# S5 stage of a decoder step: output-side complex products accumulated on TensorE, doubled columns for B and C, x scaled on ScalarE

## The chip, the cores and the metric

The kernel runs on 1 core of one Trainium2 chip, in one launch. Its time is the device time of one execution in microseconds (us). The core has five engines that run side by side, each with its own instruction queue: TensorE (PE, matrix products and transposes), VectorE (DVE), ScalarE (ACT), GpSimd (POOL) and SyncE (SP, which here only issues transfers). They wait for one another through semaphores.

## The reference, cut to what matters

One inference step of a decoder over 256 prompt tokens and 8 sequences of 8 new tokens (320 tokens in all, width 1024). The first layer is an S5 layer: a complex diagonal state space for each of 64 groups of 16 channels, with 64 states to a group. Later parts (memory attention, a squared-ReLU MLP, a latent-attention layer, another memory attention and MLP) are not touched.

```python
def s5_mixer(u, a_re, a_im, log_dt, b_re, b_im, c_re, c_im, d_skip, w_glu, h0_re, h0_im):
    ...
    mag = jnp.exp(ar * dt)
    abar_re = mag * jnp.cos(ai * dt)
    abar_im = mag * jnp.sin(ai * dt)
    ...
    bbar_re = coef_re[..., None] * br - coef_im[..., None] * bi
    bbar_im = coef_re[..., None] * bi + coef_im[..., None] * br
    bu_re = jnp.einsum('gnk,btgk->btgn', bbar_re, ug)
    bu_im = jnp.einsum('gnk,btgk->btgn', bbar_im, ug)
    ...
    _, _, h_re, h_im = lax.associative_scan(
        _complex_affine_combine, (a_seq_re, a_seq_im, bu_re, bu_im), axis=1)
    y = jnp.einsum('gkn,btgn->btgk', cr, h_re) - jnp.einsum('gkn,btgn->btgk', ci, h_im)
    y = y.reshape(bsz, t, dm) + d_skip.astype(f32) * u.astype(f32)
    g = jax.nn.gelu(y, approximate=False).astype(u.dtype)
    z = g @ w_glu
    out = z[..., :dm] * jax.nn.sigmoid(z[..., dm:])
    return out, h_re[:, -1], h_im[:, -1]
```

Beside it stands `mem_kv`, which projects 256 memory tokens to keys and values of the first layer (`mn @ w_k`, `mn @ w_v`); it depends on nothing of the S5 layer.

## The kernel before, in words

The 320 tokens are cut into chunks of L = 8 steps, which gives NCH = 40 chunks. Inside a chunk the state space is written out as matrix products; between chunks a scan carries the state. The 64 groups are worked in four quarters (`hq` 0 to 3) of 16 groups each, with an upper and a lower half (`hh`) on partitions 0 to 63 and 64 to 127.

**Parameters.** `natb` and `natc` hold B and C by rows. `transposed` (L818) turns them by TensorE into `bcps` and writes them out as `m_b` and `m_c`, with halves copied by ScalarE (L827) and VectorE (L829 to L834). The input `xc` is scaled by `rC` on VectorE (L804, four tiles `xr`), turned (`ups`) and kept as `U`.

**State side** (`state_side`, L879): for each quarter and half, two products and a sum on VectorE (L885 to L887, tiles `tq`), a column of it kept in `bz` by ScalarE (L889), transposes `rps`, their copies `rt` by ScalarE (L894), and 32 small products `sps` with `U`, which ScalarE copies into the scan's array `H` (L904, L905).

**Output side** (`out_side`, L908): for each quarter and half, two products and a sum on VectorE, `ca` or for the third quarter `hca` (L923), `ct` (L924) and their sum (L925); `ct` has one buffer. TensorE multiplies the sum with `bz` (`kps`, L932), ScalarE copies it out as `kk` (L935), VectorE adds the diagonal `dd` (L941), and eight transfers of the SP queue spread `kk` over a tile `tt` (L944).

**Scan** (`scan`, L948): `scan(0)` works on the first two quarters, `scan(1)` on the last two. Each is a tree of small operations on VectorE (`sc` and `H`, L961 to L967), and ends with copies into the tile `HS` (L982, L984 on VectorE, the rest on ScalarE). Here HS(0) and HS(1) are these two tiles.

**Outputs** (`outputs`, L987): for each quarter 16 pairs of products, `yps<-tt,U` (L999) and `yps<-ca,HS` (L1001), then transposes `ytp`, a Gelu, and a split into `xh` and `xl`, the inputs of the GLU. The GLU is a product with `w_glu` in three matmuls a piece (L204 to L206) on chunks of weights: `wraw` is loaded by the SP queue (L183), ScalarE makes `whi` of it (L190) and VectorE `wlo` (L191). After the GLU come the sigmoid and the product `y` (L649). `fps` are transposes for the final states; `kn`, `kt` and `xps` belong to what follows the GLU.

**Fillers.** `mem_kv` of the first layer is 128 matmuls of 256 columns (L567, L569, `mm<-mnp,...`) whose weights lie raw in the three weight rings `raw`, `hi` and `lo` of `weight_buffers`, without being split; each ring has two buffers of one pool, listed twice, and a third one from the pool `wg`, which opens after `mem_kv`.

The instructions of an engine run in the order in which they were queued. That order is not the order of the code: a scheduler decides it when the program is built, from the dependencies, the buffers that come free and its own estimates. So an edit in one place can move work of another.

Of the kernel before, what the change touches and what calls it, by code (L numbers as in the profile page):

```python
# [88 lines left out]
class Trunk:  # L89
# [76 lines left out]

    def weight_buffers(self, third):
        self.wring = {k: [(self.wp, 2), (self.wp, 2), (third, 1)] for k in ('raw', 'hi', 'lo')}

# [8 lines left out]
    def load_chunk(self, srcs, cols):  # L178
# [13 lines left out]
        return hi, lo  # L192

    def load_plain(self, src):

        kind = ('raw', 'hi', 'lo')[self.plain % 3]
        self.plain += 1
        raw = self.wtile(kind, F32)
        self.last_w = self.nc.sync.dma_start(raw.rearrange("p (k c) -> p k c", c=256), src)
        return raw  # L200
# [188 lines left out]
    def load_gains(self, pool):  # L389
        nc, I, cp = self.nc, self.I, self.cp  # L390
        self.gT = cp.tile([128, 128], F32, name="gT")
        gn = pool.tile([109, 128], F32, name="gn")
        for i, g in enumerate(GAINS):
            nc.sync.dma_start(gn[i * 16:(i + 1) * 16, :], I[g].rearrange("l (j p) -> (l j) p", p=128))
        nc.sync.dma_start(gn[96:104, :], I['kv_in_norm'].rearrange("(j p) -> j p", p=128))
        nc.sync.dma_start(gn[104:106, :], I['kv_latent_norm'].rearrange("(j p) -> j p", p=128))
        nc.sync.dma_start(gn[106:109, :], I['q_norm'].rearrange("l (j p) -> (l j) p", p=128))
        ps = self.ps_mm.tile([128, 512], F32, name="gps", tag="mm")
        self.transpose(ps[:, :109], gn)
        nc.vector.tensor_copy(self.gT[:, :109], ps[:, :109])  # L400
# [147 lines left out]
    def mem_kv(self, l, op, x):  # L548
# [6 lines left out]
        for g in range(8):  # L555
            W, c0 = (Wk, g * 256) if g < 4 else (Wv, (g - 4) * 256)
            ps = [self.ps_mm.tile([128, 512], F32, name="mm", tag="mm") for _ in range(2)]
            for k0 in range(0, KD, 4):
# [13 lines left out]
                for kk in range(4):  # L572
                    k = k0 + kk
                    for b in range(2):
# [3 lines left out]
                        else:  # L578
                            s = slice(kk * 256, (kk + 1) * 256)
                            ms = slice(b * 128, (b + 1) * 128)  # L580
                            self.mm3(ps[b][:, :256], xh[:, k, ms], xl[:, k, ms], hi[:, s], lo[:, s], k == 0, k == KD - 1)
            t = op.tile([128, 512], F32, name="kvo", bufs=1)
            if g < 4:
# [28 lines left out]
    def s5(self, mkv):  # L612
        sp, close_sp = self.open("s5")
        mn, close_mn = self.open("memn0", side="right")
        mx = self.mem_x(mn, plain=True)
        self.rB = mn.tile([128, MT], F32, name="rB")
        close_s8 = self.s5_scan(sp, mkv, mx)
        for unit, _ in enumerate(self.mem_kv(0, mkv, mx)):
            if unit == 0:
                with self.tc.issue_after(self.last_w.ins):  # L620
                    self.load_gains(sp)
        close_mn()
        wg, self.close_wg = self.open("wglu", side="right")
        self.weight_buffers(wg)
        close_s8()
        close_sp()
# [32 lines left out]
    def s5_scan(self, sp, mkv, mx):  # L659
# [15 lines left out]
        for i in range(2):  # L675
# [6 lines left out]
        bn = xp.tile([2 * G, 1024], F32, name="bn", tag="xr", bufs=2)  # L682
        nat = {'b': pp.tile([2 * G, (K + 1) * N], F32, name="natb"),
               'c': self.xp.tile([2 * G, (K + 1) * N], F32, name="natc", tag="xl", padded_shape=[128, 2560])}

# [8 lines left out]
        for i in range(2):  # L694
            cols = slice(i * D // 2, (i + 1) * D // 2)
            nc.sync.dma_start(xc[i * NCH:i * NCH + NC_P], I['x_prompt'][0].rearrange("(c s) d -> c s d", s=L)[:, :, cols])
            nc.sync.dma_start(xc[i * NCH + NC_P:(i + 1) * NCH], I['x_sample'][:, :, cols])
        load_nat('c', nat['c'][:, :K * N])
        V.tensor_copy(an[:, 2], ld[:, :, None].to_broadcast([G, 2, N]))

        V.tensor_mul(nat['b'][:, :K * N].rearrange("p (k n) -> p n k", k=K),
                             bn.rearrange("p (n k) -> p n k", k=K), gxn[:, None, :].to_broadcast([2 * G, N, K]))
        for t in nat.values():
            V.tensor_copy(t[:, K * N:], t[:, :N])
        V.tensor_mul(dn, dn, gxn[:G])
# [80 lines left out]
        self.par_done = V.tensor_sub(rev(QY), T1, T2)  # L786
        a8n = sp.tile([128, 2, G], F32, name="a8n")
        A.activation(a8n[:, 0], PR[:, 8], AF.Copy)
# [13 lines left out]
        for fb in range(4):  # L802
            xr = xp.tile([2 * NCH, 8, L, K], F32, name="xr", bufs=2)
            V.tensor_mul(xr, xc[:, :, fb * 128:(fb + 1) * 128].rearrange("p s (g k) -> p g s k", k=K),  # L804
                                 rC[:, None, :, None].to_broadcast([2 * NCH, 8, L, K]))
            for half in range(2):
# [10 lines left out]

        def transposed(c):  # L818
            t = nat[c]
            ev = mat[c].rearrange("p r g (k o) -> p o k r g", o=2)  # L820
            for o in range(2):
                for x0 in (0, 4):
                    p = tp("bcps")
                    for x in range(4):
                        self.transpose(p[:, x * 128:(x + 1) * 128], t[:, (2 * (x0 + x) + o) * N:(2 * (x0 + x) + o + 2) * N])
                    v = p.rearrange("p (k r g) -> p k r g", k=4, r=2)
                    A.activation(ev[top, o, x0:x0 + 4], v[top], AF.Copy)  # L827
                    if o == 0:
                        V.tensor_copy(ev[bot, 1, x0:x0 + 4], v[bot])  # L829
                    elif x0 == 0:  # L830
                        V.tensor_copy(ev[bot, 0, 1:5], v[bot])
                    else:
                        V.tensor_copy(ev[bot, 0, 5:], v[bot, :3])
                        V.tensor_copy(ev[bot, 0, 0], v[bot, 3])  # L834
# [73 lines left out]
        def out_side(hq):  # L908
            ca = []
            E = V  # L910
            if hq == 2:
                big = self.hp.tile([128, 2, 8, 9, K], F32, name="hca", tag="h", padded_shape=[128, 2, 8, 10, K])
            for hh in range(2):
# [7 lines left out]
                A.activation(c[bot, :, 0], CI[bot, gs], AF.Copy, scale=-1.0)  # L921
                t1 = s8.tile([128, 8, L, K], F32, name="ct", bufs=1)
                E.tensor_mul(c[:, :, 1:], b4(CR, gs), q4(X1, gs))  # L923
                E.tensor_mul(t1, b4(CI, gs), q4(Y1, gs))  # L924
                E.tensor_add(c[:, :, 1:], c[:, :, 1:], t1)  # L925

            kk = s8.tile([K, L, 16, K], F32, name="kk", tag="kk", bufs=1)
            ps = at("kps")
            for j in range(4):
                for q in range(4):  # L930
                    u = q * 4 + j
                    nc.tensor.matmul(ps[q * 32:q * 32 + K, j * 128:(j + 1) * 128], bz[:, (hq * 16 + u) * K:(hq * 16 + u + 1) * K],  # L932
                                     ca[u // 8][:, u % 8, 0:L, :], start=True, stop=True, skip_group_check=True)
            for q in range(4):
# [8 lines left out]
            for s in range(L):  # L943
                nc.sync.dma_start(tt[s * K:(s + 1) * K, s:], kk[:, 0:L - s])  # L944
            return ca, tt

# [856 lines left out]
```

## Time and profile before

| quantity | value |
|---|---|
| time, median of 3 runs | 1229.59 us (1228.91 to 1232.15) |
| the profiled execution's own time | 1235.15 us |
| its span, first to last instruction | 1233.5 us |
| mean granted TensorE clock | 0.966 of full speed |
| busy share of TensorE, VectorE, ScalarE, GpSimd | 92%, 59%, 44%, 15% |
| the S5 stage with its GLU | the first 229.7 us of the span |

The busy shares are means over the whole span and hide how the first stage differs: there TensorE waits for VectorE, while from some 150 us on it is nearly always busy. The rows below are from that stage. In a timeline row the first number is the start, the second the time from the first to the last end of the group; a bracket names the idle time of the engine just before it and what ended that time.

### The profile page before, as it was taken

How to read it: one execution, taken by the hardware profiler on the slowest of the kernel's cores; microseconds unless marked ns; L12 is line 12 of the kernel's file. 1: busy time of each engine (PE TensorE's matmuls, PEld its weight loads, DVE VectorE, ACT ScalarE, POOL GpSimd, SP SyncE). 2: the span in 40 equal slices, each digit the busy share in tenths (PEclk: the TensorE clock that was granted, in tenths of full speed). 3: DMA queues.
4: the chain of work that ended last, by engine and by line, in shares of the span. 5: the costliest groups of instructions: out<-in, count | busy, mean ns of one | idle time of the engine just before them, and what ended most of it. 6: DMA issues, size and time to landing. Idle time of an engine off the chain costs nothing.

```text
span 1233.5 us, 21037 instructions
## 1 busy us (share of the span) xinstructions
PE 1139.3 (92%) x8105; PEld 1026.6 (83%) x8105; DVE 726.7 (59%) x1266; ACT 546.7 (44%) x992; POOL 182.3 (15%) x190
## 2 busy tenths in 40 slices
PE   4997699889988999999989999998999899999996
PEld 3886599776787999999979984578967899999996
DVE  5998944664468553564587674416843685435543
ACT  6344454534444543453366353224443365335541
POOL 2000000350027000000050054202700140000011
PEclk8999799999998999999999999989999999999998
DMA  8535358637334445454443565437272434454441
GB/s 165 180 100 116 72 118 289 245 120 269 124 103 126 137 154 153 143 151 152 154 143 104 170 185 153 140 137 268 84 272 94 137 99 144 151 153 139 155 149 49
DMA packets 151233, 184.84 MB, mean 150 GB/s; under 512 B 16719, under 2 KB 119388, under 8 KB 151068
## 3 DMA queue, kind: packets, MB, share of 16 engines
q1 hardware_dynamic: 141660, 174.84, 46.3%
q10 hardware_dynamic: 6976, 5.46, 1.4%
q0 software_dynamic: 2496, 3.20, 0.9%
q8 instruction: 64, 1.05, 0.3%
q14 instruction: 37, 0.30, 0.1%
HBM read 174.89 MB, written 6.21 MB: 147 GB/s over the span
## 4 chain that ended last, share of the span: by engine, by line
PE 75%; DVE 10%; DMA 5%; SPq 3%; issue 2%; ACT 2%; POOL 2%; POOLq 0%; DVEq 0%; ACTq 0%
PE mm L205 17%; PE mm L204 17%; PE mm L206 17%; PE kt L102 2%; PE sps L1182 2%; PE mm L567 2%; DVE xl L279 2%; PE s L1662 2%; SPq L944 2%; DVE wlo L191 1%; DMA natc<-in_ssm_c_im 1%; PE pov L1239 1%; PE s L1703 1%; PE pps L1217 1%; PE mm L569 1%
## 5 line engine op out<-in xcount | busy, mean ns | idle before, releaser
L191 DVE TENSOR_TENSOR wlo<-wraw,whi 128x1024 fp32r<-128x1024 f32 (+1 forms) x206 | 252.9, 1232 | 279.3 <-ACT whi L190 269.1
L190 ACT ACTIVATE whi<-wraw 128x1024 fp32r<-128x1024 f32 (+1 forms) x216 | 224.5, 1044 | 302.8 <-PE mm L205 246.6
L205 PE MATMUL mm<-xl,whi 128*128 128x320 f32 x944 | 296.8, 317 | 9.1 <-DVE xl L279 7.0
L204 PE MATMUL mm<-xh,whi 128*128 128x320 f32 x944 | 280.6, 318 | 12.7 <-ACT t_up L1295 3.6
L206 PE MATMUL mm<-xh,wlo 128*128 128x320 f32 x944 | 287.3, 314 | 0.0
L205 PEld LDWEIGHTS mm<-xl,whi 128*128 128x128 f32 x944 | 181.8, 193 | 13.7 <-DVE xl L279 9.6
L204 PEld LDWEIGHTS mm<-xh,whi 128*128 128x128 f32 x944 | 175.9, 192 | 16.8 <-ACT t_up L1295 3.9
L206 PEld LDWEIGHTS mm<-xh,wlo 128*128 128x128 f32 x944 | 179.7, 192 | 0.1
L204 PE MATMUL mm<-hh,whi 128*128 128x320 f32 x512 | 158.2, 309 | 0.0
L205 PE MATMUL mm<-hl,whi 128*128 128x320 f32 x512 | 158.0, 309 | 0.0
L206 PE MATMUL mm<-hh,wlo 128*128 128x320 f32 x512 | 157.1, 308 | 0.0
L205 PEld LDWEIGHTS mm<-hl,whi 128*128 128x128 f32 x512 | 96.1, 188 | 0.0
L204 PEld LDWEIGHTS mm<-hh,whi 128*128 128x128 f32 x512 | 96.1, 188 | 0.0
L206 PEld LDWEIGHTS mm<-hh,wlo 128*128 128x128 f32 x512 | 95.9, 188 | 0.0
L118 POOL TENSOR_TENSOR sq<-sq 128x320 f32<-128x320 f32 x34 | 41.4, 1219 | 204.1 <-ACT sq L120 203.4
L191 POOL TENSOR_TENSOR wlo<-wraw,whi 128x1024 fp32r<-128x1024 f32 x10 | 25.4, 2538 | 286.4 <-ACT whi L190 198.1
L102 PEld LDWEIGHTS kt<-ident,kn 128*128 128x128 f32 x256 | 28.9, 143 | 22.2 <-issue 5.8
L102 PE MATMUL kt<-ident,kn 128*128 128x128 f32 x256 | 38.1, 283 | 8.6 <-ACT ktb L1109 3.2
L1591 POOL DMA_DIRECT2D rop<-in_cache_k_rope x64 | 34.5, 540 | 37.4 <-issue 20.4
L256 POOL TENSOR_TENSOR t_up<-y,rr 128x320 f32<-128x320 f32 x6 | 7.5, 1258 | 219.2 <-DVE h L257 219.2
L1107 DVE COPY ktb<-kt 128x512 f32<-128x512 f32 x32 | 22.0, 687 | 21.0 <-PE kt L102 20.9
L1109 ACT ACTIVATE ktb<-kt 128x512 f32<-128x512 f32 x32 | 19.1, 596 | 31.4 <-PE kt L102 26.0
(495 smaller groups left out, 1958.6 us busy)
## 6 DMA issues: line engine op xcount, KB each, us to landing
wraw<-in_w_mlp_up SPq DMA_DIRECT2D x64, 512.0 KB, 4.2
wraw<-in_w_mlp_down SPq DMA_DIRECT2D x64, 512.0 KB, 3.5
kn<-in_cache_mem_k SPq DMA_DIRECT2D x16, 1024.0 KB, 7.3
vn<-in_cache_mem_v SPq DMA_DIRECT2D x16, 1024.0 KB, 9.1
wraw<-in_w_glu SPq DMA_DIRECT2D x32, 256.0 KB, 4.1
wraw<-in_w_mem_q SPq DMA_DIRECT2D x16, 512.0 KB, 5.3
wraw<-in_w_mem_o SPq DMA_DIRECT2D x16, 512.0 KB, 5.0
lat<-in_cache_kv_latent SPq DMA_DIRECT2D x64, 128.0 KB, 2.5
```

The lines of the kernel that those rows point to most:

```text
L102: self.nc.tensor.transpose(out, in_, self.ident[b:b + k, b:b + k])
L118: eng.tensor_add(st['acc'], st['acc'], st['last'])
L190: nc.scalar.activation(hi[:, :cols], raw[:, :cols], AF.Copy)
L191: (nc.gpsimd if self.chunk in POOL_LO else nc.vector).tensor_sub(lo[:, :cols], raw[:, :cols], hi[:, :cols].bitcast(F32))
L204: nc.tensor.matmul(ps, wh, xh, start=start, stop=False)
L205: nc.tensor.matmul(ps, wh, xl, start=False, stop=False)
L206: nc.tensor.matmul(ps, wl, xh, start=False, stop=stop)
L279: lo = nc.vector.scalar_tensor_tensor(xl[:, j, :], s, gpre(j), xh[:, j, :].bitcast(F32), op0=ALU.mult, op1=ALU.subtract)
L567: nc.tensor.matmul(ps[b][:, :MT], w[:, bs], xh[:, k, :], start=k == 0, stop=k == KD - 1)
L944: nc.sync.dma_start(tt[s * K:(s + 1) * K, s:], kk[:, 0:L - s])
L1182: nc.tensor.matmul(sps[h * 32:(h + 1) * 32, :MT], qm[:, h * 2 + db, j * 128 + i * 32:j * 128 + (i + 1) * 32], ktb[:, h * 2 + db, :], start ...
L1591: last[eng] = eng.dma_start(dst, src[bass.ds(v, 1)].rearrange("o p d -> (o p) d"))
```

## The change

Four things are edited.

1. On the output side the sum of the two products is no longer formed. `ca` and `ct` stay as two tiles (`ct` with four buffers), and each of the two users multiplies twice into the same PSUM tile: `kps` has a second matmul of 112 columns with `ct`, and `yps` a third pair, `yps<-ct,HS`.
2. `natb` and `natc` are laid out with each column block twice, so that a transpose gives both halves on all 128 partitions, and ScalarE copies them out in 8 pieces instead of VectorE and ScalarE in halves. C is loaded into a tile `cn` first and then copied into `natc`, once by VectorE and once by ScalarE.
3. `xr` is scaled by 32 ScalarE instructions of 80 x 128 instead of four VectorE ones of 80 x 1024.
4. The staging tile `kvo` of `mem_kv` takes a buffer of a weight ring (`plain_tile`; it shows as `wlo` in the rows of the change), and the rings get a third buffer for `raw` and `hi` only.

```diff
-    def weight_buffers(self, third):
-        self.wring = {k: [(self.wp, 2), (self.wp, 2), (third, 1)] for k in ('raw', 'hi', 'lo')}
+    def weight_buffers(self, third, kinds=('raw', 'hi', 'lo')):
+        self.wring = {k: [(self.wp, 2), (self.wp, 2)] + [(third, 1)] * (k in kinds) for k in ('raw', 'hi', 'lo')}
...
-            t = op.tile([128, 512], F32, name="kvo", bufs=1)
+            t = op.tile([128, 512], F32, name="kvo", bufs=1) if l else self.plain_tile()
...
-        self.weight_buffers(wg)
+        self.weight_buffers(wg, ('raw', 'hi'))
...
+        A.activation(nat['b'][:, :, 1], nat['b'][:, :, 0], AF.Copy)
...
-            V.tensor_mul(xr, xc[:, :, fb * 128:(fb + 1) * 128].rearrange("p s (g k) -> p g s k", k=K),
-                                 rC[:, None, :, None].to_broadcast([2 * NCH, 8, L, K]))
+            for i in range(L):
+                A.activation(xr[:, :, i], xc[:, i, fb * 128:(fb + 1) * 128].rearrange("p (g k) -> p g k", k=K),
+                             AF.Copy, scale=rC[:, i:i + 1])
...
+            ev = mat[c].rearrange("p r g k -> p k r g")
+            for k0 in range(0, K, 4):
+                p = tp("bcps")
+                for x in range(4):
+                    self.transpose(p[:, x * 128:(x + 1) * 128],
+                                   t[:, k0 + x].rearrange("p o n -> p (o n)"))
+                v = p.rearrange("p (k r g) -> p k r g", k=4, r=2)
+                A.activation(ev[:, k0:k0 + 4], v, AF.Copy)
...
+        V.tensor_copy(nat['c'][:, :, 0], cnv)
+        A.activation(nat['c'][:, :, 1], cnv, AF.Copy)
...
-                t1 = s8.tile([128, 8, L, K], F32, name="ct", bufs=1)
+                t1 = s8.tile([128, 8, L, K], F32, name="ct", bufs=4)
+                cb_.append(t1)
                 E.tensor_mul(c[:, :, 1:], b4(CR, gs), q4(X1, gs))
                 E.tensor_mul(t1, b4(CI, gs), q4(Y1, gs))
-                E.tensor_add(c[:, :, 1:], c[:, :, 1:], t1)
...
-                                     ca[u // 8][:, u % 8, 0:L, :], start=True, stop=True, skip_group_check=True)
+                                     ca[u // 8][:, u % 8, 0:L, :], start=True, stop=False, skip_group_check=True)
+                    nc.tensor.matmul(ps[q * 32:q * 32 + K, j * 128 + K:(j + 1) * 128], bz[:, (hq * 16 + u) * K:(hq * 16 + u + 1) * K],
+                                     cb_[u // 8][:, u % 8, 0:L - 1, :], start=False, stop=True, skip_group_check=True)
...
-                    for st in range(2):
+                    for st in range(3):
...
-                                nc.tensor.matmul(o, HS[:, g2 * NCH:g2 * NCH + 64], ca[hh][:, gl, 1:, :], start=False, stop=True)
+                                m = ca[hh][:, gl, 1:, :] if st == 1 else cb_[hh][:, gl]
+                                nc.tensor.matmul(o, HS[:, g2 * NCH:g2 * NCH + 64], m, start=False, stop=st == 2)
```

The scheduler answers with another order of the whole first stage. Three places of it follow; the line numbers of the change are 2 to 5 higher than those before.

On VectorE, at the start of `scan(0)`, the kernel before queues scan operations, the sums into `ca`, the additions to `kk` and the state side of the last quarters in turn:

```order
L923 TENSOR_TENSOR ca<-m_c,X_211 128x8x128
L982 COPY HS<-H 64x16x8
L984 COPY HS<-H 64x16x8
L925 TENSOR_TENSOR ca<-ca,ct 128x8x128
L965 TENSOR_TENSOR sc<-sc 128x256
L965 TENSOR_TENSOR sc<-sc 128x16x8
L941 TENSOR_TENSOR kk<-kk,dd 16x128 x2
L886 TENSOR_TENSOR tq<-m_b,QY 128x1024
L924 TENSOR_TENSOR ct<-m_c,Y_212 128x1024
```

In the change the state side runs ahead of the scan, and the four `ct` tiles of the first two quarters are made in one go just before it:

```order
L888 TENSOR_TENSOR tq<-m_b,QY 128x1024
L889 TENSOR_TENSOR tq<-tq 128x1024
L887 TENSOR_TENSOR tq<-m_b,QX 128x1024
L869 MEMSET H 128x64
L927 TENSOR_TENSOR ct<-m_c,Y_212 128x1024 x2
L944 TENSOR_TENSOR dd<-dT,ident 16x128 x2
L927 TENSOR_TENSOR ct<-m_c,Y_212 128x1024 x2
L981 MEMSET HS 128x24
L591 TENSOR_TENSOR kt<-mm,rB 128x256
L926 TENSOR_TENSOR ca<-m_c,X_211 128x8x128
```

Of the seven `ct` and six sums that stood ahead of HS(0), four `ct` are left there; the third quarter's two `ct` now stand near the end of `scan(1)`, 68 rows after HS(0).

On TensorE, behind the outputs of the second quarter, the kernel before goes on with the GLU:

```order
L1001 MATMUL yps<-ca,HS 64x128 x2
L999 MATMUL yps<-tt,U 64x128 x2
L1001 MATMUL yps<-ca,HS 64x128 x2
L204 MATMUL mm<-xh,whi 128x320 x4
L932 MATMUL kps<-ca,bz 16x128 x2
L205 MATMUL mm<-xl,whi 128x320
L206 MATMUL mm<-xh,wlo 128x320
```

In the change matmuls of `mem_kv` stand between the outputs instead. This is the place behind the first quarter's outputs, where the `kps` of the third quarter needs its `ct`:

```order
L1006 MATMUL yps<-ct,HS 64x128 x2
L934 MATMUL kps<-hca,bz 16x128
L572 MATMUL mm<-whi,mnp 128x256 x7
L572 MATMUL mm<-wraw,mnp 128x256 x5
L102 MATMUL ytp<-ident,yc 128x128 x8
L1003 MATMUL yps<-tt,U 64x128 x2
L1006 MATMUL yps<-ca,HS 64x128 x2
L936 MATMUL kps<-ct,bz 16x112
```

And this is where the GLU begins, behind the last matmuls of `mem_kv`:

```order
L1006 MATMUL yps<-ct,HS 64x128 x2
L572 MATMUL mm<-wraw,mnp 128x256 x3
L572 MATMUL mm<-whi,mnp 128x256 x8
L102 MATMUL ytp<-ident,yc 128x128 x8
L102 MATMUL fps<-ident,H 32x128
L102 MATMUL fps<-ident,F 32x128 x8
L207 MATMUL mm<-xh,whi 128x320
L208 MATMUL mm<-xl,whi 128x320
```

In the kernel before all 128 matmuls of `mem_kv` stand ahead of the first `yps<-ca,HS`; in the change 73 do, and 55 behind it (12, then 18, 14 and 11 between the outputs), and no matmul of the GLU is left between the outputs.

On the SP queue the kernel before has two of the transfers of `w_glu` behind the `tt` of the first quarter, and ten behind those of the second:

```order
L944 DMA tt<-kk 16x768
L944 DMA tt<-kk 16x512
L944 DMA tt<-kk 16x256
L183 DMA wraw<-in_w_glu 128x2x256 x10
L944 DMA tt<-kk 16x2048
L944 DMA tt<-kk 16x1792
```

In the change (with buffer numbers) all of them stand behind the last `tt`, and the chunk 1877, which the GLU multiplies first, behind 1908 and 1939:

```order
L948 DMA tt_242<-kk_1246 16x512
L948 DMA tt_242<-kk_1246 16x256
L183 DMA wraw_1908<-in_w_glu 128x2x256 x2
L183 DMA wraw_1939<-in_w_glu 128x2x256 x2
L183 DMA wraw_1877<-in_w_glu 128x2x256 x2
```

Each of these three waits for TensorE to be done with the matmuls of `mem_kv` that read the buffer before.

## Rows read from the trace of the kernel before

**Rows 1.** Windows of core 0: length, busy us of each engine (instructions), PEclk, DMA
```profile
25.20:131.90 106.70, 88.92 (x734) 75.48 (x735) 98.24 (x211) 47.55 (x114) 0.00 (x0) 0.92 0.49 137
131.60:229.70 98.10, 90.95 (x787) 85.99 (x788) 50.95 (x126) 49.00 (x86) 1.80 (x1) 0.95 0.63 184
```

**Rows 2.** VectorE by shape, 25 to 132 us: count | busy us, mean ns | idle before
```profile
L924 DVE TENSOR_TENSOR ct<-m_c,Y 128x1024 f32<-128x1024 f32 x7 | 8.4, 1204 | 0.0
L925 DVE TENSOR_TENSOR ca<-ca,ct 128x1024 f32<-128x1024 f32 x4 | 4.8, 1209 | 0.0
L804 DVE TENSOR_TENSOR xr<-xc,rC 80x1024 f32<-80x1024 f32 x4 | 4.8, 1224 | 0.0
...
L191 DVE TENSOR_TENSOR wlo<-wraw,whi 128x1024 fp32r<-128x1024 f32 x3 | 3.6, 1214 | 3.1 <-ACT whi L190 3.1
...
L829 DVE COPY m_c<-bcps 64x512 f32<-64x512 f32 x2 | 2.1, 1030 | 0.1
...
L833 DVE COPY m_c<-bcps 64x384 f32<-64x384 f32 x1 | 0.8, 805 | 0.0
```

**Rows 3.** Timeline of VectorE, at the C load and at the end of HS(0)
```profile
25.14 0.20 DVE L704 COPY natc<-natc 128x64 f32<-128x64 f32 x1 [3.36 <-DMA natc<-in_ssm_c_im]
...
27.71 0.22 DVE L765 TENSOR_TENSOR W<-W 128x64 f32<-128x64 f32 x1
...
102.05 1.21 DVE L886 TENSOR_TENSOR tq<-m_b,QY 128x1024 f32<-128x1024 f32 x1
103.19 1.21 DVE L924 TENSOR_TENSOR ct<-m_c,Y 128x1024 f32<-128x1024 f32 x1
...
131.50 0.42 DVE L984 COPY HS<-H 64x512 f32<-64x512 f32 x1
```

**Rows 4.** Timeline of TensorE: mem_kv, first outputs, kps, ytp, outputs at full clock
```profile
48.98 3.62 PE L567 MATMUL mm<-mnp,whi 128*128 128x256 f32 x16
52.43 0.72 PE L102 MATMUL ups<-ident,xr 80*128 80x80 f32 x8
...
131.61 1.11 PE L1001 MATMUL yps<-ca,HS 128*64 128x128 f32 x6 [14.24 <-DVE HS L982]
132.49 0.66 PE L999 MATMUL yps<-tt,U 128*64 128x128 f32 x4
...
136.64 1.07 PE L932 MATMUL kps<-hca,bz 128*16 128x128 f32 x32
137.64 1.09 PE L102 MATMUL ytp<-ident,yc 128*128 128x128 f32 x8
...
139.15 0.39 PE L999 MATMUL yps<-tt,U 128*64 128x128 f32 x4
139.37 0.39 PE L1001 MATMUL yps<-ca,HS 128*64 128x128 f32 x4
```

**Rows 5.** TensorE by line, 131.6 to 229.7 us
```profile
L204 PE MATMUL mm<-xh,whi 128*128 128x320 f32 x128 | 37.7, 316 | 1.4 <-ACT xh L96 1.3
L999 PE MATMUL yps<-tt,U 128*64 128x128 f32 x120 | 13.7, 293 | 2.4 <-DMA tt<-kk 2.2 <-ACT kk L935 0.2
```

**Rows 6.** Scan operations on VectorE, 131.9 to 160 us, first and last of four
```profile
L967 DVE TENSOR_TENSOR H<-H,sc 128x16 f32<-128x16 f32 (+7 forms) x18 | 5.3, 296 | 0.0
...
L965 DVE TENSOR_TENSOR sc<-sc 128x16 f32<-128x16 f32 (+7 forms) x17 | 4.3, 251 | 0.0
```

**Rows 7.** The page's transfers: KB each, us to landing
```profile
wraw<-in_w_glu SPq DMA_DIRECT2D x32, 256.0 KB, 4.1
```

**Rows 8.** ScalarE by shape, up to 132 us
```profile
L827 ACT ACTIVATE m_c<-bcps 64x512 f32<-64x512 f32 x4 | 4.1, 1032 | 1.9 <-PE bcps L102 1.9
...
L190 ACT ACTIVATE whi<-wraw 128x1024 fp32r<-128x1024 f32 x3 | 3.2, 1058 | 11.2 <-DMA wraw<-in_w_glu 11.2
...
L889 ACT ACTIVATE bz<-tq 128x128 f32<-128x128 f32 x8 | 2.5, 310 | 3.5 <-DVE tq L887 2.9 <-DVE ca L923 0.5
```

**Rows 9.** Timeline of ScalarE: copies of 256 columns with a scale pointer
```profile
19.55 1.15 ACT L542 ACTIVATE mnp<-mps,gmT 128x256 f32<-128x256 f32 x3
```

More of the change, by code (lines that the diff above doesn't have):

```diff
@@ L192, in load_chunk, with plain_tile, load_plain @@
         return hi, lo
-    def load_plain(self, src):
+    def plain_tile(self):
         kind = ('raw', 'hi', 'lo')[self.plain % 3]
         self.plain += 1
-        raw = self.wtile(kind, F32)
+        return self.wtile(kind, F32)
+    def load_plain(self, src):
+        raw = self.plain_tile()
         self.last_w = self.nc.sync.dma_start(raw.rearrange("p (k c) -> p k c", c=256), src)
@@ L391, in load_gains @@
         self.gT = cp.tile([128, 128], F32, name="gT")
-        gn = pool.tile([109, 128], F32, name="gn")
+        gn = pool.tile([109, 128], F32, name="gn", tag="a8n", padded_shape=[128, 128])
         for i, g in enumerate(GAINS):
@@ L682, in s5_scan @@
         bn = xp.tile([2 * G, 1024], F32, name="bn", tag="xr", bufs=2)
-        nat = {'b': pp.tile([2 * G, (K + 1) * N], F32, name="natb"),
-               'c': self.xp.tile([2 * G, (K + 1) * N], F32, name="natc", tag="xl", padded_shape=[128, 2560])}
+        cn_ = xp.tile([2 * G, 1024], F32, name="cn", tag="xr", bufs=2)
+        nat = {'b': pp.tile([2 * G, K, 2, N], F32, name="natb"),
+               'c': self.xp.tile([2 * G, K, 2, N], F32, name="natc", tag="xl", padded_shape=[128, 20, 2, 64])}
         def load_nat(c, t):
@@ L697, in s5_scan @@
             nc.sync.dma_start(xc[i * NCH + NC_P:(i + 1) * NCH], I['x_sample'][:, :, cols])
-        load_nat('c', nat['c'][:, :K * N])
+        load_nat('c', cn_)
         V.tensor_copy(an[:, 2], ld[:, :, None].to_broadcast([G, 2, N]))
[L701 to L704, printed above, removed]
+        V.tensor_mul(nat['b'][:, :, 0].rearrange("p k n -> p n k"),
+                     bn.rearrange("p (n k) -> p n k", k=K), gxn[:, None, :].to_broadcast([2 * G, N, K]))
+        A.activation(nat['b'][:, :, 1], nat['b'][:, :, 0], AF.Copy)
         V.tensor_mul(dn, dn, gxn[:G])
@@ L786, in s5_scan @@
         self.par_done = V.tensor_sub(rev(QY), T1, T2)
-        a8n = sp.tile([128, 2, G], F32, name="a8n")
+        a8n = sp.tile([128, 2, G], F32, name="a8n", tag="a8n", bufs=1)
         A.activation(a8n[:, 0], PR[:, 8], AF.Copy)
@@ L819, in transposed @@
             t = nat[c]
[L820 to L834, printed above, removed]
+            ev = mat[c].rearrange("p r g k -> p k r g")
[6 more added lines that the diff above has]
+                A.activation(ev[:, k0:k0 + 4], v, AF.Copy)
         transposed('b')
+        cnv = cn_.rearrange("p (k n) -> p k n", k=K)
+        V.tensor_copy(nat['c'][:, :, 0], cnv)
+        A.activation(nat['c'][:, :, 1], cnv, AF.Copy)
         transposed('c')
@@ L908, in out_side @@
         def out_side(hq):
-            ca = []
+            ca, cb_ = [], []
             E = V
@@ L944, in out_side @@
                 nc.sync.dma_start(tt[s * K:(s + 1) * K, s:], kk[:, 0:L - s])
-            return ca, tt
+            return ca, cb_, tt
         def scan(f):
@@ L985, in scan, with outputs @@
             return HS
-        def outputs(hq, HS, ca, tt):
+        def outputs(hq, HS, ca, cb_, tt):
             yc = sp.tile([128, L, 8, K], F32, name="yc", tag="tmp4", bufs=3)
```

## The prediction

> **What bounds the kernel now.** I read the windows first. From 25.2 to 131.9 us, where HS(0) is finished, VectorE is busy for 98.2 of 106.7 us and TensorE for 88.9; after that, up to the end of the GLU, TensorE is busy for 91.0 of 98.1 us and VectorE for half of them [rows 1]. So there are two regimes. Ahead of HS(0) the chain of VectorE sets the time: TensorE has run out of other work and sits idle for 14.2 us until the HS copies let `yps<-ca,HS` start [rows 4]. Behind HS(0) TensorE's own work sets the time, and every matmul that is added or pushed behind that point is paid in full. The groups of VectorE then say what can be saved in the first regime [rows 2], the timeline of TensorE what a matmul costs in the second [rows 4].
>
> The sum below is made in the profiled execution, which took 1235.15 us with a span of 1233.5; that is 5.6 us above the median of the three runs. I carry only the difference over to the median.
>
> **HS(0) comes earlier.** A VectorE operation of 128x1024 takes 1.14 us from start to start (102.05 to 103.19) [rows 3]. Ahead of HS(0) these fall away or move behind it:
> - six sums (four `ca`, two `hca` of the same shape): 6.8 us;
> - three `ct` of the seven [rows 2], now queued in `scan(1)`: 3.4 us;
> - four `xr` [rows 2], now on ScalarE: 4.6 us;
> - three `wlo` [rows 2], since no GLU weight is loaded so early: 3.4 us;
> - after the C load, seven copies out of `bcps`: the first two of 1.03, the last of the longer ones 0.8, together 5.4 us [rows 2];
> - eight small parameter operations that stood behind the copy that waits for C (25.14, after 3.36 us of waiting) and end at 27.9; with two of the copies taken off they are some 1.6 us [rows 3], and now stand ahead of that wait;
> - the idle time, 106.7 - 98.2 = 8.5 us [rows 1], of which 3.1 us was a wait for `whi` [rows 2].
>
> That is 33.7 us, and HS(0) would be ready at 98.2. Three things are added, none of which the trace shows. The `natc` copy of 128x1024 on VectorE lies between 0.42 us (an HS copy of half the columns on half the partitions [rows 3]) and 1.14; I take 0.7. The `m_c` copies on ScalarE are now the last thing ahead of the first `hca`; VectorE waits for none to four of them, 0 to 4.1 us at 1.03 each [rows 8], and I take two, 2.1. The additions to `kk` waited in the kernel before too; with the order shown above I put 1.5 us back, of 0 to 3. HS(0) is then at 102.5, bounds 98.5 to 106.5: **29 us earlier** than before.
>
> TensorE is not late for that: before HS(0) it loses 55 matmuls of `mem_kv` and gains 32 short `kps`.
>
> **What TensorE has to do behind it.**
> - `mem_kv`: 16 records took 52.43 - 48.98 = 3.45 us [rows 4]. A matmul of 256 columns shows as two records, so it takes 0.43 us, and 55 of them are 23.8 us. They filled the time before HS(0) and now stand behind it.
> - `yps<-ct,HS`: four records of a pair of matmuls took 139.37 - 139.15 = 0.22 us [rows 4], 0.108 each: 64 are 6.9 us.
> - `kps<-ct`: 32 records, 16 matmuls, took 1.0 us [rows 4], 0.063 each with 128 columns. With 112 columns it lies between nothing and that; seven eighths of the columns speak for the upper end, which I take. The 32 of the last two quarters stand behind HS(0): 2.0 us. The other 32 are hidden ahead of it.
>
> **New waits.** (1) The `kps` of the third quarter needs `ct`, and VectorE makes that only near the end of `scan(1)`. Its 68 scan operations before sum to 18.9 us of durations in four groups of which two are shown [rows 6]; they overlap by some 0.08 us each, so 13.5, less about 1 for those behind `ct`; with two `ca` and two `ct` at 1.14 that is 17.0 us after HS(0). TensorE has until then 48 `yps` (5.2), 12 matmuls of `mem_kv` (5.2), eight `ytp` (1.1 [rows 4]) and a few more `yps` (0.4). It also starts slowly after its wait, as before: there six records take the 0.88 us from 131.61 to 132.49, 0.15 each against 0.055 at 139.15 [rows 4]; I put 1.5 us for the whole slow start. That is 13.4 and leaves a stall of **3.6 us**, bounds 0 to 5; behind it the `kk` of that quarter, eight transfers and the `tt` follow, but 14 us of `yps` and `mem_kv` lie in between and hide them. (2) The GLU's first chunk, 1877, goes into a buffer that the last matmuls of `mem_kv` read. From its release 4.1 us pass to landing [rows 7], 0.5 for the second issue, and 1.06 for `whi` [rows 8]; ahead of the GLU stand 17 transposes, 2.2 us. That leaves 3.5 us; the release comes a few matmuls earlier, and I take **2.8**, bounds 0 to 4. ScalarE and VectorE queue `whi` and `wlo` of the next chunks behind it, but nobody waits for those first. For a stretch of low clock after stall (1) I add 0.7 us (0 to 1.5); that of (2) replaces the one after the `tt` wait.
>
> **Waits that go.** The GLU no longer runs beside the outputs, so TensorE's waits for `tt` and `kk` (2.4) and for `xh` (1.4) [rows 5] go: 3.8 us. The GLU's own matmuls, transposes and the wait for `kn` stay.
>
> **Sum:** -29.4 + 23.8 + 6.9 + 2.0 + 3.6 + 2.8 + 0.7 - 3.8 = +6.6 us. Most of what VectorE saves is spent twice: `mem_kv` was free cover for a wait that TensorE had anyway, and the added products run where TensorE is the bound. I take +6, as two of the stalls may overlap with gaps that TensorE has already: 1241 us in the profiled execution, **1235.5 us** in the median.
>
> **A rule on the other side.** The 32 pieces of `xr` on ScalarE are not in the trace. Three copies of 256 columns with a scale pointer take 1.15 us, 0.35 to 0.38 each [rows 9]; one of 128 columns without a pointer shows 0.31 alone [rows 8]. I take 0.28 between 0.20 and 0.35, so 9.0 us on ScalarE for 4.6 us on VectorE. They stand ahead of the first `bz` copies, which VectorE's ring of three `tq` buffers waits for; with 16 pieces ahead of the first (4.5 us) VectorE has about 4.5 us of other work, so at 0.28 it costs nothing.
>
> The Trainium skill, ScalarE: Activation LUTs, section "Rules for kernel authors", says to use VectorE rather than ScalarE for multiplications; its section "What ACT_TABLE_LOAD costs" gives 186 ns plus 0.833 ns a column, 93 ns more for a pointer operand, and 93 ns of overlap back to back, from which I estimate 0.29 us a piece and 9.4 us for all. By that estimate the sum would be as mine; by the rule the move itself is a loss, which is rival D.
>
> **Rivals.**
> - *B, faster.* VectorE's chain ahead of HS(0) is shorter still. For: VectorE is 92% busy there [rows 1], so all that is taken off counts, and with none of the three added waits HS(0) is at 98.5. Against: it takes another 5 us to get a gain that can be measured; I know of only one place, the wait of 3.4 us for C [rows 3]. It decides at HS(0) before 93; at 92 the time is 1225.
> - *C, the same.* Both new stalls are hidden, because `scan(1)` is faster than its durations say and the first chunk's buffer is free earlier. Then 3.6 + 2.8 + 0.7 go: 1228.5. For: the 3.6 is a difference of two sums of 17 and 13. Against: each stands in the order.
> - *D, ScalarE becomes the bound* of the state side, as the pieces take 0.35 or the `rt` and `bz` copies queue behind them: 2.2 us more for the pieces and as much for VectorE's ring, HS(0) 4.5 us later, 1240. For: ScalarE's 47.6 busy us [rows 1] grow by 9 in a third of that window. Against: more than half of it is free.
>
> **How the numbers follow.** A forecast (1232 to 1239) 0.42, D 0.17, C 0.25, B 0.16. No change that can be told means within 0.3%, 3.7 us. That gives faster 0.16, same 0.25, slower 0.59. The range reaches from between B and C, 1226, to D with a stall at its upper bound, 1243; half of B and a little beyond D are left out.
>
> **What would show it.** In the changed profile: HS(0) copies near 102 to 103; 55 matmuls of `mem_kv` between the outputs; TensorE idle before `kps<-ct` of the third quarter, released by VectorE, for some 3.6 us; TensorE idle before the first matmul of the GLU, released by ScalarE's `whi`, for some 2.8; `y` of the GLU some 6 us later; the same times from there on. The prediction is wrong if HS(0) is ready before 95 or after 108, if TensorE has no stall behind it, or if what follows the GLU changes by itself.

## The result, and the profile after

The change makes the kernel slower: a median of 1236.22 us (20 runs) against 1230.61 us for the kernel before in the same session (20 runs), a ratio of 1.0051 with a 95% interval of 1.0036 to 1.0066. That is 5.6 us; 5.9 were forecast. The profiled execution has a span of 1241.7 us against 1233.5, 8.2 us more; it was the slowest of the change's 20, 7.1 us above their median, as the one before lies 4.5 us above its own.

The windows of the changed kernel, in the columns of [rows 1]; the first ends with HS(0):

```profile
25.20:106.80 81.60, 66.92 (x668) 58.10 (x669) 73.48 (x179) 53.05 (x140) 0.00 (x0) 0.90 0.35 87
107.00:165.00 58.00, 56.33 (x654) 49.07 (x653) 26.43 (x91) 21.96 (x45) 1.80 (x1) 1.00 0.46 105
165.00:180.00 15.00, 11.88 (x64) 10.82 (x63) 7.00 (x12) 7.41 (x15) 0.00 (x0) 0.77 0.59 183
```

The regimes are as they were. VectorE needs 73.5 busy us up to HS(0) where it needed 98.2 [rows 1]; then TensorE is busy nearly all the time. VectorE's timeline has the copy of C, the end of HS(0) and the last product of the GLU:

```profile
26.76 0.69 DVE L837 COPY natc<-cn 128x1024 f32<-128x1024 f32 x1 [6.35 <-DMA cn<-in_ssm_c_im]
...
106.42 0.43 DVE L988 COPY HS<-H 64x512 f32<-64x512 f32 x1
...
236.85 0.49 DVE L652 TENSOR_TENSOR y<-mm,t_up 128x320 f32<-128x320 f32 x1 [4.43 <-PE mm L209]
```

HS(0) is ready at 106.85, 25.1 us earlier than before, and yet the GLU's last `y` starts at 236.85, where it started at 229.72 in the trace before: 7.1 us of the 8.2 are already there at that point. TensorE in between:

```profile
105.12 0.44 PE L102 MATMUL kps<-ident,kt 128*128 128x128 f32 x2 [1.23 <-DVE kt L591]
105.40 1.03 PE L572 MATMUL mm<-wraw,mnp 128*128 128x256 f32 x4
106.27 0.38 PE L102 MATMUL kps<-ident,kt 128*128 128x128 f32 x2
106.48 2.76 PE L572 MATMUL mm<-wraw,mnp 128*128 128x256 f32 x12
109.08 0.59 PE L572 MATMUL mm<-whi,mnp 128*128 128x256 f32 x2
109.60 0.44 PE L1003 MATMUL yps<-tt,U 128*64 128x128 f32 x4
109.87 0.39 PE L1006 MATMUL yps<-ca,HS 128*64 128x128 f32 x4
110.09 0.39 PE L1006 MATMUL yps<-ct,HS 128*64 128x128 f32 x4
...
123.34 0.27 PE L936 MATMUL kps<-ct,bz 128*16 128x112 f32 x1 [1.12 <-DVE ct L927]
...
124.48 0.27 PE L936 MATMUL kps<-ct,bz 128*16 128x112 f32 x1 [0.54 <-DVE ct L927]
...
168.08 0.30 PE L102 MATMUL fps<-ident,H 128*32 128x128 f32 x1 [0.96 <-ACT gt L1015]
168.72 1.03 PE L102 MATMUL fps<-ident,F 128*32 128x128 f32 x8 [0.34 <-ACT ca L1061]
171.57 0.64 PE L207 MATMUL mm<-xh,whi 128*128 128x320 f32 x1 [1.82 <-ACT whi L190]
```

The 14 us of idle time at 131.61 [rows 4] are gone: `mem_kv` stands in front of the first `yps<-ca,HS`, which now starts 3 us after HS(0), at the pace of full clock. The waits for `ct` and for the GLU's first chunk are there, with 1.7 and 1.8 us (and 1.3 ahead of `fps`). The wait for `tt` that the kernel before had [rows 5] is gone.

### The profile page after: what moved, and what is told of

Its sections match the earlier page's. It is cut to its first block, busy times and chain, and to the rows that moved or that the text cites. A ratio compares the mean times of both kernels' runs of the same rounds, so it can differ in the third digit from the quotient of the medians.

```text
span 1241.7 us, 21568 instructions
## 1 busy us (share of the span) xinstructions
PE 1153.6 (93%) x8361; PEld 1042.4 (84%) x8361; DVE 703.5 (57%) x1243; ACT 557.2 (45%) x1026; POOL 181.1 (15%) x190
## 4 chain that ended last, share of the span: by engine, by line
PE 79%; DVE 8%; DMA 4%; ACT 4%; issue 2%; POOL 2%; SPq 1%; POOLq 0%; ACTq 0%; DVEq 0%
PE mm L208 18%; PE mm L207 18%; PE mm L209 18%; PE kt L102 2%; PE sps L1187 2%; PE s L1667 2%; PE mm L572 2%; PE mm L570 1%; DMA xc<-in_x_sample 1%; PE pov L1244 1%; PE ops L1202 1%; PE s L1708 1%; DMA wraw<-in_w_mem_q 1%; DVE wlo L191 1%; PE pps L1222 1%
## 5 line engine op out<-in xcount | busy, mean ns | idle before, releaser
L207 PE MATMUL mm<-xh,whi 128*128 128x320 f32 x944 | 286.4, 319 | 11.7 <-ACT t_up L1300 3.6
L207 PEld LDWEIGHTS mm<-xh,whi 128*128 128x128 f32 x944 | 179.3, 194 | 14.9 <-ACT whi L190 4.9
L1302 DVE TENSOR_TENSOR t_up<-t_up 128x320 f32<-128x320 f32 x64 | 31.1, 507 | 1.8 <-ACT hh L1301 1.7
L1303 DVE TENSOR_TENSOR hl<-t_up,hh 128x320 fp32r<-128x320 f32 x64 | 31.1, 508 | 1.0
```

Source lines behind the costliest of these rows:

```text
L207: nc.tensor.matmul(ps, wh, xh, start=start, stop=False)
L1302: V.tensor_mul(a, a, a)
L1303: V.tensor_sub(hl[b // 4][:, b % 4, :], a, hh[b // 4][:, b % 4, :].bitcast(F32))
```

## The experiments

One theory stood against several rivals. M is the account of the prediction, that the time behind the first `yps<-ca,HS` is TensorE's own work, so that the added products and every matmul of `mem_kv` that stands there are paid in full. K says that the weight ring shared with `kvo` is the loss, X that ScalarE's scaling is, P that the products alone are, L that whatever shortens VectorE's chain is gained, W that `mem_kv` counts wherever it stands. Ratios are to the kernel before, measured beside each run, with their 95% intervals. The fourth part of the change also puts the small tiles `gn` and `a8n` into one buffer; that stays in every version that is made from the change.

**The sum put back.**

```diff
+                E.tensor_add(c[:, :, 1:], c[:, :, 1:], t1)
...
-                    for st in range(3):
+                    for st in range(2):
```

> The change with its first part undone: the sum of the two products is formed on VectorE again, ct has one buffer, kps and yps have no extra matmuls; doubled columns, xr on ScalarE and kvo in the weight ring stay. Theory M (what is lost is TensorE's work behind HS(0): the added products, 8.9 us, and mem_kv pushed there): 29 instead of 55 mem_kv matmuls stand behind HS(0) here and the added products are gone, against an HS(0) some 7 us later, so about 9 us less than the change: 1225 to 1230. Theory K (the weight ring shared with kvo holds mem_kv back): within 2 us of the change, about 1236. Theory X (ScalarE's scaling delays the state side): within 2 us of the change too.

1229.16 us, 0.9989 (0.9969 to 1.0009): the change's loss is gone with its first part. K and X, which both expected it to stay, fall as accounts of this loss. VectorE's chain ends later than in the change, 111.6 plus 0.4, and TensorE is done much earlier:

```profile
111.59 0.42 DVE L987 COPY HS<-H 64x512 f32<-64x512 f32 x1
...
222.02 0.49 DVE L652 TENSOR_TENSOR y<-mm,t_up 128x320 f32<-128x320 f32 x1 [4.43 <-PE mm L209]
```

`y` is 7.7 us earlier than before, the median only 1.4 to 1.9; behind the GLU this trace takes 1007.2 us to its end and that of before 1003.8. Over all traces of this study that rest lies between 997 and 1008 us. It follows TensorE's granted clock: behind the last `y` the clock is at its lower level (1.2 GHz) for 33 to 61 us of a trace, and the more, the longer the rest (correlation 0.91 over the 14 traces; 61 us in the longest, 37 us in the shortest). So a few us of each time go with the clock behind the GLU; what moves it there, no run varied.

**kvo in its own buffer, three `ct`.**

```diff
-            t = op.tile([128, 512], F32, name="kvo", bufs=1) if l else self.plain_tile()
+            t = op.tile([128, 512], F32, name="kvo", bufs=1)
...
-                t1 = s8.tile([128, 8, L, K], F32, name="ct", bufs=4)
+                t1 = s8.tile([128, 8, L, K], F32, name="ct", bufs=3)
```

> The change with kvo in a buffer of its own again, so that mem_kv's weights have six buffers instead of four; for the room, ct has three buffers instead of four. 42 instead of 55 mem_kv matmuls stand behind HS(0), 5.6 us. Theory M: 3 to 5 us less than the change, but not below the kernel before, as the added products stay: 1231 to 1234. Theory K: the whole loss comes back, 1229 or less. Theory X: no change, 1236.

1263.03 us, 1.0254 (1.0224 to 1.0283), which nobody expected. HS(0) is ready at 97.9, the earliest of all full kernels. But the groups of TensorE from 139 to 262 us show a wait that the change does not have:

```profile
L1003 PE MATMUL yps<-tt,U 128*64 128x128 f32 x96 | 13.2, 357 | 18.2 <-DMA tt<-kk 17.5 <-ACT yc L1007 0.7
```

What is late is `kk`, and ahead of it `ct`. Without the sum a `ct` tile is held until the `yps<-ct,HS` of its quarter have read it. With three buffers the second `ct` of each later quarter can be made only when the outputs of the quarter before have read theirs, and then `kps`, `kk`, the transfers and `tt` follow, one after the other. VectorE's timeline has the two waits, and SP's has the transfers:

```profile
151.71 2.36 DVE L927 TENSOR_TENSOR ct<-m_c,Y 128x1024 f32<-128x1024 f32 x2 [9.98 <-PE yps L1006]
...
158.61 0.27 DVE L945 TENSOR_TENSOR kk<-kk,dd 16x128 f32<-16x128 f32 x1
...
176.05 1.23 DVE L927 TENSOR_TENSOR ct<-m_c,Y 128x1024 f32<-128x1024 f32 x1 [13.79 <-PE yps L1006]
...
182.06 0.28 DVE L945 TENSOR_TENSOR kk<-kk,dd 16x128 f32<-16x128 f32 x1 [0.94 <-ACT kk L939]
```

```profile
140.20 18.92 SPq L183 DMA_DIRECT2D wraw<-in_w_glu  x7
159.17 6.23 SPq L948 DMA_DIRECT2D tt<-kk  x8
...
182.40 6.08 SPq L948 DMA_DIRECT2D tt<-kk  x8
```

Transfers of `w_glu` do stand ahead of `tt` on the queue, but they do not hold it up: each `tt` goes out within 0.3 us of its last `kk`. The change, with four `ct`, has such a wait once (4.04 us, at 134.66), and `mem_kv` covers it on TensorE. So this run varied two things, and the second made the loss; it is a test of neither M nor K.

**xr on VectorE again.**

```diff
-            for i in range(L):
-                A.activation(xr[:, :, i], xc[:, i, fb * 128:(fb + 1) * 128]..., AF.Copy, scale=rC[:, i:i + 1])
+            V.tensor_mul(xr, xc[:, :, fb * 128:(fb + 1) * 128]..., rC[:, None, :, None].to_broadcast([2 * NCH, 8, L, K]))
```

> The change with xr scaled on VectorE again (four multiplies), all else as changed. Theory M: VectorE's chain ahead of HS(0) grows by up to 4.6 us, of which TensorE, which arrives at the outputs 2.8 us after HS(0), feels 2: 1238. Theory K: the same, 1237 to 1239. Theory X: the wait of VectorE and TensorE for ScalarE goes, 2 us or more less: 1234 or below.

1238.65 us, 1.0060 (1.0036 to 1.0085), not to be told from the change. HS(0) is at 106.15 here. X falls; moving the scaling is neutral. M's number is met, but not for its reason, as HS(0) does not come later. On ScalarE the pieces of the change take 0.30 us each (16 in 4.79, 8 in 2.45), 0.29 from start to start:

```profile
46.49 4.79 ACT L809 ACTIVATE xr<-xc,rC 80x128 f32<-80x128 f32 x16 [4.11 <-DVE rC L741]
...
53.64 2.45 ACT L809 ACTIVATE xr<-xc,rC 80x128 f32<-80x128 f32 x8
```

**The sum put back and kvo in its own buffer** (the edits of the first two, with one `ct`).

> The change with its first and fourth part undone: sum on VectorE, kvo in its own buffer and a third buffer in each weight ring; doubled columns and xr on ScalarE stay. Theory M: like the run with only the first part undone, within 2 us, since the same 29 mem_kv matmuls stand behind HS(0): 1225 to 1230. Theory K: 5 us or more below that run. Theory X: at 1230 or above, since the scaling stays on ScalarE.

1228.57 us, 0.9977 (0.9960 to 0.9994): the fastest version that does all the work, by little. M holds; K's 5 us beyond the first experiment do not show.

**The doubled columns alone**, on the kernel before.

> The kernel before with only the second part of the change: B and C with doubled columns, copied out by ScalarE; sum, xr and kvo as before. 34 of the 128 mem_kv matmuls are queued behind HS(0). Theory M counts three terms, when HS(0) comes, 0.43 us for each mem_kv matmul behind it, and the added products: HS(0) about 10 to 12 us earlier, 14.6 us of mem_kv behind it, none added: 1230 to 1234. Rival L (what shortens VectorE's chain is gained, wherever mem_kv stands): 1220 to 1224.

1231.61 us, 1.0010 (0.9989 to 1.0032). VectorE's chain is 19.7 us shorter (HS(0) at 112.27), where M had expected 10 to 12; TensorE starts the outputs only at 116.69, and nothing of the gain reaches the end: L falls.

**The products alone**, on the kernel before, with two `ct`.

> The kernel before with only the first part of the change, the products accumulated on TensorE and no sums; ct has two buffers, for which there is room. All 128 mem_kv matmuls stand ahead of HS(0). Theory M: HS(0) 7 to 10 us earlier, added products 8.9 us, a wait for ct of up to 4: 1230 to 1235. Rival L: 1221 to 1224. Rival P (the loss of the change is the products alone, however the rest stands): 1237 or more.

1267.87 us, 1.0300 (1.0268 to 1.0331). Here all of `mem_kv` is ahead of HS(0), so none of it stands between the outputs to cover a wait, and two `ct` buffers hold the tiles of one quarter alone. The wait is that of the second experiment, longer. The SP queue (start, time to issue, count), VectorE's `ct` and `kk`, and the matmul that waits:

```profile
96.05 6.55 SPq L946 DMA_DIRECT2D tt<-kk  x8
102.70 20.48 SPq L183 DMA_DIRECT2D wraw<-in_w_glu  x12
141.94 30.00 SPq L946 DMA_DIRECT2D tt<-kk  x16
```

```profile
133.07 2.38 DVE L925 TENSOR_TENSOR ct<-m_c,Y 128x1024 f32<-128x1024 f32 x2
...
141.59 0.28 DVE L943 TENSOR_TENSOR kk<-kk,dd 16x128 f32<-16x128 f32 x1
...
158.86 2.36 DVE L925 TENSOR_TENSOR ct<-m_c,Y 128x1024 f32<-128x1024 f32 x2 [16.67 <-PE yps L1003]
...
182.83 2.36 DVE L925 TENSOR_TENSOR ct<-m_c,Y 128x1024 f32<-128x1024 f32 x2 [12.09 <-PE yps L1003]
```

```profile
149.92 0.48 PE L1001 MATMUL yps<-tt,U 128*64 128x128 f32 x2 [9.82 <-DMA tt<-kk]
```

The twelve transfers of `w_glu` are issued by 123.2, and from there the queue itself waits 18.7 us for the second quarter's `kk`. TensorE waits for `tt` for 24.1 us in all, and its clock is at the lower level for 42 us between the first product with HS(0) and the last `y` (10 us in the kernel before). The number is above P's bound, but not for P's reason: the added matmuls are 8.9 us, the waits and the slow stretches are the rest. So what the products cost by themselves can't be read from this run.

**The products and kvo in the ring**, on the kernel before, and **kvo in the ring alone**.

> The kernel before with the first and the fourth part, products accumulated with four ct buffers and kvo in the weight ring; natb, natc and xr as before. 65 mem_kv matmuls stand behind HS(0). Theory M: HS(0) some 20 us earlier, 28 us of mem_kv and 8.9 of products behind it, 4 us of waits gone: 1238 to 1245. Rival L: 1222 or less. Rival P: the same as with the products alone, within 2.

1257.06 us, 1.0196 (1.0165 to 1.0226). No theory gave that. `yps<-ca,HS` starts at 117.0, some 5 us later than M had assumed; with that, the work behind it fits up to the last `y`, 18.8 us later than before (table below). Another 4.3 us of this trace come behind the GLU, where it has the longest rest of all. With four `ct` there is no wait for `tt`.

> The kernel before with only the fourth part: kvo takes a buffer of the weight ring, the rings get a third buffer for two kinds only. 32 mem_kv matmuls stand behind HS(0), 13.9 us. Theory M: HS(0) up to 6 us earlier (no wlo ahead of it), so 1235 to 1240. Rival P and rival L: 1229 to 1232, since no work is added and VectorE's chain is the same.

1242.65 us, 1.0092 (1.0067 to 1.0118): with no work added and VectorE's chain 7.3 us shorter, 11 us are lost, 2.7 more than M's upper bound. P and L fall. So the shared ring does cost here, though it does not in the first experiment. The 32 matmuls that moved behind HS(0) are 13.9 us, M's price, and the wait for `tt` doubles to 4.1 us. The first of the moved ones stand in front of the outputs:

```profile
126.26 1.46 PE L572 MATMUL mm<-whi,mnp 128*128 128x256 f32 x6
127.65 0.44 PE L1004 MATMUL yps<-ca,HS 128*64 128x128 f32 x4
```

**Half of `mem_kv` left out**, in the kernel before and in the change; the same edit in both.

```diff
-            for k0 in range(0, KD, 4):
+            for k0 in range(0, KD if xl is not None else 4, 4):
```

> The kernel before with half of the first layer's mem_kv left out (64 of its 128 matmuls and half of its weight loads; its keys and values are then sums over half the width). All 64 stand ahead of HS(0), where TensorE waits for VectorE. Theory M: these matmuls are covered, so the time falls by 3 us at most: 1227 to 1231. Rival W (mem_kv's work counts wherever it stands): 27.7 us less, 1203 or so.

> The change with half of the first layer's mem_kv left out, as in the run before this one. 9 instead of 55 of its matmuls stand behind HS(0), 19.9 us less. Theory M: the time falls by 15 to 22 us against the change, to 1214 to 1221, unless the transfers of tt, which then have less work in front of them, open a wait. Rival W: 27.7 us less, 1208. If what stands behind HS(0) is hidden anyway: within 4 us of the change, 1232 to 1240.

This pair decides. Before: 1229.43 us, 0.9987 (0.9965 to 1.0010), so 64 matmuls of 0.43 us, 27.7 us of TensorE's work, show next to nothing in the time. They were not quite free: in this trace VectorE idles for 2.1 us up to HS(0) where it idled for 8.5 [rows 1], HS(0) is 8.0 us earlier and the last `y` 9.7; the two spans keep 5.6 of that (1227.9 against 1233.5) and the medians 2.0. After: 1218.97 us, 0.9895 (0.9847 to 0.9943), 17 us below the change (1236.22; 19 by the two ratios), for 46 matmuls fewer behind HS(0), 19.9 us. From the first product with HS(0) to the last `y` the halved change is 20.3 us shorter than the change, the halved kernel before only 1.7 us shorter than before. W falls, and so would any theory by which that place is hidden. The outputs of the halved kernel before, and the outputs and the last `y` of the halved change:

```profile
123.59 1.11 PE L1001 MATMUL yps<-ca,HS 128*64 128x128 f32 x6 [6.37 <-DVE HS L982]
```

```profile
106.84 0.39 PE L1006 MATMUL yps<-ca,HS 128*64 128x128 f32 x4
```

```profile
213.58 0.49 DVE L652 TENSOR_TENSOR y<-mm,t_up 128x320 f32<-128x320 f32 x1 [4.43 <-PE mm L209]
```

**The sum on GpSimd**, first on the version with the sum put back and kvo in its own buffer, then on the kernel before; two `ct` in both.

```diff
-                E.tensor_add(c[:, :, 1:], c[:, :, 1:], t1)
+                nc.gpsimd.tensor_add(c[:, :, 1:], c[:, :, 1:], t1)
```

> Second and third part of the change, with the sum kept but formed on GpSimd, which is idle in this stage (eight additions of 128x1024, two ct buffers); kvo in its own buffer. No product is added to TensorE and no sum is left on VectorE. 42 mem_kv matmuls stand behind HS(0). Theory M: HS(0) near 109, 18 us of mem_kv behind it, so 5 to 7 us below the kernel before, 1224 to 1227. If GpSimd's additions slow VectorE or come late for kps: 1230 or more.

> The kernel before with only the sum moved to GpSimd and two ct buffers. All 128 mem_kv matmuls stand ahead of HS(0). Theory M: HS(0) up to 6.8 us earlier and nothing behind it: 1224 to 1228. If the twelve transfers of GLU weights ahead of the third tt block the SP queue, as in the run with the products alone: 1245 or more.

1241.72 us, 1.0097 (1.0059 to 1.0135), and 1234.36 us, 1.0025 (1.0006 to 1.0045). M's numbers are missed, since HS(0) is hardly earlier than with the sum on VectorE: 117.35 against 116.3, and 131.08 against 131.92. GpSimd and VectorE get into each other's way, as the two timelines of the first of them show:

```profile
68.74 7.11 POOL L928 TENSOR_TENSOR ca<-ca,ct 128x1024 f32<-128x1024 f32 x2 [60.98 <-DMA hn<-in_cache_ssm_im]
```

```profile
71.04 2.59 DVE L964 TENSOR_TENSOR sc<-H,a8r 128x256 f32<-128x256 f32 x1
73.56 2.57 DVE L965 TENSOR_TENSOR sc<-H,a8i 128x256 f32<-128x256 f32 x1
...
77.33 0.41 DVE L964 TENSOR_TENSOR sc<-H,a8r 128x256 f32<-128x256 f32 x1
```

While GpSimd's sums run, some of the scan operations take 2.6 us instead of 0.41.

**One table for all.** For each trace: the start of the first matmul with HS(0), that of the last `y`, the time between, and what is left of it when `mem_kv` behind HS(0) (0.433 us a matmul) and the added products (8.9 us) are taken off.

| kernel | first product with HS(0) | last `y` | between | mem_kv behind | left |
|---|---|---|---|---|---|
| before | 131.61 | 229.72 | 98.1 | 0 | 98.1 |
| change | 109.87 | 236.85 | 127.0 | 55 | 94.3 |
| sum put back | 114.03 | 222.02 | 108.0 | 29 | 95.4 |
| kvo own, three ct | 107.78 | 259.70 | 151.9 | 42 | 124.8 |
| xr on VectorE | 107.73 | 233.05 | 125.3 | 55 | 92.6 |
| sum put back, kvo own | 118.32 | 224.14 | 105.8 | 29 | 93.3 |
| doubled columns alone | 116.69 | 228.65 | 112.0 | 34 | 97.2 |
| products alone | 119.89 | 264.47 | 144.6 | 0 | 135.7 |
| products, kvo in ring | 117.00 | 248.52 | 131.5 | 65 | 94.5 |
| kvo in ring alone | 127.65 | 239.38 | 111.7 | 32 | 97.9 |
| half mem_kv, before | 123.59 | 220.03 | 96.4 | 0 | 96.4 |
| half mem_kv, change | 106.84 | 213.58 | 106.7 | 9 | 93.9 |
| sum on GpSimd | 120.30 | 234.33 | 114.0 | 42 | 95.8 |
| sum on GpSimd, before | 130.78 | 232.30 | 101.5 | 0 | 101.5 |

In twelve of fourteen what is left is 92.6 to 101.5 us, where "between" itself runs from 96.4 to 131.5; the other two are those with the added products and fewer than four `ct`, with 17.5 and 24.1 us of waits for `tt` and slow stretches behind them. In none of the 14 traces is `tt` held up by the queue: all its 56 groups are issued within 0.3 us of their last `kk`. So M's account carries from the start of the outputs on, to within some 4.5 us. The 8.9 us of the products are not measured by themselves: with products and four `ct` 92.6 to 94.5 us are left, without products 93.3 to 101.5, so they may be a few us too dear, or waits may have gone. What M doesn't give is when the outputs start, which the scheduler's order decides anew with each edit, and whether `ct` comes too late. Its range was met in six of the twelve runs (sum put back, `xr` on VectorE, sum put back with kvo own, doubled columns alone, and the two halves).

## Why the prediction was right

The forecast was 1235.5 us, and the mechanism was the one that was named. That the number came so close is in part luck: the outputs start 21.7 us earlier than before, not the 29 that the sum took off, and the waits and slow stretches behind them came out about as much smaller.

- *HS(0) earlier by 29 us, at 102.5:* 25.1, at 106.85, just beyond the upper bound of 106.5. What falls away was right, and so was the price of the `natc` copy, 0.69 against 0.7. VectorE's 73.5 busy us are as reckoned. What failed is the idle time: I took all 8.5 us off and allowed 3.6 new ones, and VectorE idles for 8.1 of 81.6 us. C landed 1.6 us later (the first copy of it starts between 23.3 and 26.8 us over all traces), and 2.4 us are waits for `rps`, which I had put at nothing. The wait for `m_c` was 1.4 (2.1 taken), those at `kk` 2.1 (1.5 taken).
- *"TensorE is not late for that":* this step failed. The first product with HS(0) starts at 109.87, 3 us after HS(0), since `mem_kv` matmuls and two transposes that wait for `kt` stand in front. With it went the slow start that I had added (1.5 us): TensorE came busy.
- *`mem_kv` behind HS(0), 23.8 us:* right. The pair with half of it left out shows the place both ways, nearly free before and paid after.
- *Added products, 8.9 us:* the price of `yps` holds: a group of four records starts every 0.22 us (109.87 to 110.09). The total is not measured by itself.
- *Wait for `ct`, 3.6 us:* there, at the place named, but 1.7, since TensorE came later.
- *GLU's first chunk, 2.8 us:* 1.8 and another 1.3 ahead of `fps`. The slow stretch behind it, a mean clock of 0.77 over 15 us, costs some 3.4 us by that share, where I had let it replace the old one. Behind the wait for `ct`, for which I had added 0.7 us of low clock, there is none: the clock is 1.00 from 107 to 165.
- *Waits that go, 3.8 us:* right, and the one for `kn`, 2.5 us in the trace before, which I had left standing, went too.
- *The sum to the last `y`:* +6 forecast, +7.1 measured. Another 1.1 us come behind it, which is less than the rest differs from trace to trace. The 5.6 us of the medians are the firmer number.

The rivals: B needed HS(0) before 93; it did not come before 97 in any full kernel. C needed both stalls hidden; they were there. D has its answer in the third experiment: 0.30 us a piece, within my bounds, and no effect on the time. The estimate from the Trainium skill (ScalarE: Activation LUTs, "What ACT_TABLE_LOAD costs"), 0.29 us a piece, is what the trace shows from start to start, better than my 0.28. The rule of that page's section "Rules for kernel authors", to keep multiplications on VectorE, does not decide here: either engine gives the same time, as the trace with VectorE has HS(0) at 106.15 and the one with ScalarE at 106.85.

What stays open: whether `mem_kv` is pushed behind HS(0) by the four weight buffers themselves or only by the order that the scheduler finds with them; what the added products cost with nothing else changed, for which four `ct` and kvo in its own buffer would be needed; and what sets the clock behind the GLU. None of these was tried.

## What to carry to other kernels

Ask first which engine sets the time at the place where work is added, not which is busiest: the change took 25 us off the stretch that VectorE sets, and paid with TensorE's time in the stretch that TensorE sets. Filler work that covers a wait is free only as long as it stands in that wait; when a buffer plan or an edit moves it behind, its full price appears (here 0.43 us a matmul, and 11 us for a buffer that was shared). And a sum that is left to the accumulation keeps its second operand alive until the last user has read it: the two worst versions here, 2.5% and 3% slower, have too few buffers for that tile, so that the next quarter's chain starts only behind the outputs of this one. It looks like a blocked transfer queue from TensorE's side, as the matmul waits for a transfer; what the transfer itself waited for tells the two apart.

## What the runs showed of the hardware

- TensorE's granted clock differs from trace to trace where TensorE has the same matmuls to do: behind the last `y` it is at the lower level (1.2 GHz) for 33 to 61 us, and that stretch takes 997 to 1008 us.
- GpSimd and VectorE slow each other on such operations: scan operations of 128x256 took 2.59 and 2.57 us while GpSimd formed sums, 0.41 after it. GpSimd's sums of 128x1024 took 2.35 us at best there, 7.11 for the two above, and 13.5 for two on the kernel before. Other VectorE operations kept their time beside them (twelve of 128x1024 took some 1.21 us each, in the last run).
